# Group 0 of the input projection: the sums of Q5's weights by accumulating transfers in place of additions on VectorE

## The chip, the cores and the metric

The kernel runs on one core of a Trainium2 chip. The metric is the device time of one execution in microseconds. Before the change the median of three runs is 1290.94 us (1290.84 to 1290.96).

The engines are named as the profile names them: PE is TensorE's matmul and PEld its weight load, DVE is VectorE, ACT is ScalarE, POOL is GpSimd, SP is SyncE. POOL and SP, and sometimes ACT, also issue DMA transfers. Each engine works through its own queue in order: an instruction that waits holds up all that stand behind it.

## The reference

The block is one layer of a diffusion transformer over 512 latent tokens of width 2048 and 256 context tokens. One input projection feeds two token mixers, attention and a 2-D Fourier mixing; their gated results are projected, merged with sigmoid gates, projected once more and added to the input. Cut to what matters:

```python
h = _modulate(_rmsnorm(xs, norm_g[l]), shift[:, None], scale[:, None])
p = h @ w_l                                   # (512 x 2048) @ (2048 x 9216)
q = _rope(_rmsnorm(_heads(p, OFF_Q, N_Q_HEADS), q_norm_g[l]), cos, sin) * q_scale
...
attn = _attention(q, jnp.concatenate([k, kc], axis=1), jnp.concatenate([v, vc], axis=1))
y = _merge(p[..., OFF_ZA:], attn, w_proj_a[l], w_proj_b[l], w_out[l])
new_xs = xs + gate[:, None] * y
...
return _rmsnorm(xs, final_g)
```

The change concerns the product h @ w_l, and of its 9216 columns the first 1024 that the kernel's groups work on (512 of the queries, 512 of the gate z_a).

## The kernel before, in words

All inputs are float32. A factor is split into two parts, hi and lo, that TensorE multiplies quickly: ACT copies the source into hi (L180), DVE subtracts hi from the source and gives lo (L181). One product is then three matmuls, hi by hi, lo by hi, hi by lo, on L338, L339 and L340. So the weights of every piece pass through ACT and DVE before TensorE can use them: hi is needed at the first of the three matmuls, lo at the second.

**Stages.** Up to about 144 us the start: adaLN's vectors, the normalized rows h, and the columns of the Fourier branch. To 156 us the Fourier transform along the tokens (tiles ah, al, fch, pd). Then eight groups of the input projection of 76 us and more each, g = 0 to 7, attention from about 810 us, the branch projections, and the output projection.

**A group** is a block product of 1024 columns by seven products instead of eight (a Strassen-Winograd form). h and the weights are cut into 2 x 2 blocks; each product multiplies a form of h (A11, Z5, A12, ...) by a form of the weights. The products run in the order P1, Q5, P2, Q6, P7, Q3, Q4. Each has four pieces of 1024 columns; one piece is 12 matmuls of 128x512. P1, Q5, Q6 and Q4 use running sums of the weight blocks: P1 the first block, Q5 the sum of two, Q6 of three, Q4 of four. P2 and Q3 use one block as it is. P7 uses the sum of three less a block that is loaded for it.

**The chain.** The running sums live in four buffers, R0 to R3, one for each piece (`chain` in the code, R_1339 to R_1342 in the rows below). L219 on SP loads the first block. To add the next block there are two ways:

- L291, a POOL transfer with `accum_op=add`, issued as soon as the piece's split has read R (`e.nxt` in `split_piece`), or
- an addition on DVE, L268, of a raw block that SP has loaded into a buffer wr (L216).

`stream_product` chooses: a step whose number stands in `by_dve` is done on DVE and takes a raw buffer, any other by L291. For the groups `BY_DVE_GATES` is (1,): step 1, from P1's sum to Q5's, is on DVE; the steps to Q6's and, behind P7, to Q4's are on POOL. P7's subtraction is L276: it reads R, which then holds three blocks, and writes the result into the raw buffer.

**Buffers.** There are six raw buffers, four in the pool wp and two in rp, which are handed out again as they come free; three pairs of hi and lo, and from Q5 of group 0 on two more pairs in tiles that h no longer needs (the s tiles 128x2x256 of the rows: s_286/s_287 and s_433/s_434 make up one pair, s_571/s_572 and s_734/s_735 the other).

**Order.** TensorE's order is written out. On DVE, ACT, POOL and SP most of the order of the groups comes from the tile framework's scheduler, which places each instruction by its own estimate of when its inputs are ready. So a change of one step moves others.

**Other work of the stretch.** L966 stores the gates of the Fourier branch (tile part) to memory (b_d) from POOL's queue; L1394 then loads a table into qr, whose memory overlaps that of part, and so waits for both stores. L944 scales the Fourier results into part, L950 and L659 belong to the same stage. L993 and L994 make the forms S2 and S4 of h on DVE. L1106 combines results of the products. L1210 to L1216 rotate the queries.

Of the kernel before, what the change touches and what calls it, by code (L numbers as in the profile page):

```python
# [60 lines left out]
BY_DVE_GATES, BY_DVE_OUT = (1,), ()  # L61
# [11 lines left out]
def context_piece(g, name, pc):  # L73

    n = 28 * (g - NQZ) + 4 * ONE_GROUP.index(name) + pc
    if n % 2 == 0 and 0 <= n < 8:
        return "cn", n // 2
    if n % 7 == 4 and 18 <= n < 46:
        return "cr", n // 7 - 2
# [43 lines left out]
def block_kernel(ctx, tc, xT, ctx_rows, ctx_toks, x, c_row, w_ss, w_gate, vecs, qkg, rope, dft_c, dft_s,  # L123
# [74 lines left out]
    def stream(key, src, *a, **k):  # L198
        todo.append(Piece(key, src if isinstance(src, list) else [src], *a, **k))
# [191 lines left out]
    def stream_product(name, g, w, by_dve, pieces=4):  # L391

        what = next(p[2] for p in PRODUCTS if p[0] == name)
        for pc in range(pieces):
            key = (name, g, pc)
            part = lambda i: w[CHAIN[i][0], CHAIN[i][1], pc]
            r = (pc + CHAIN_FROM.get(g, 0)) % 4
            if isinstance(what, tuple) and name == "P7" and g >= BRANCH_A:
                stream(key, [p7_d[g - BRANCH_A, pc]], 1024, 2, pc=r)
            elif isinstance(what, tuple):  # L400
                off = name == "P7"
                stream(key, [w[a, b, pc] for a, b in what], 1024, 2, pc=r, nxt=part(3) if off else None, off=off)
            else:
                stream(key, [part(what)] if what in by_dve else [], 1024, 2, stage=what, pc=r,
                       nxt=part(what + 1) if what < (3 if g >= BRANCH_A else 2) and what + 1 not in by_dve else None)
                todo[-1].first = part(0)
# [3 lines left out]
    def stream_keys(g):  # L410
        stream(("K", g), flat(k_d[g]), NKEY, KT, "raw")
        stream(("V", g), flat(v_d[g]), NKEY, KT, dst=lambda: tiles(g))
# [8 lines left out]
    for g in range(LAST + 1):  # L421
        for name in ONE_GROUP:
            if (g, name) == (LAST, "Q4"):
                stream_keys(0)
            if g == KV:
                f = CTX_FORMS.index(next(f for n, f, _, _ in PRODUCTS if n == name))
                stream(("cf", name), cf_d[:, :, f].rearrange("i p j c -> p i j c"), 1024, 8, dst=ctx_tiles)
            stream_product(name, g, w_g[g], BY_DVE_GATES)
            for pc in range(4):
                p = context_piece(g, name, pc)  # L430
                if p:
                    src, cols = (ctx_toks[p[1]], 1024) if p[0] == "cn" else (ctx_rows[p[1]], 4 * C)
                    stream(p, src, cols, 1, "raw")
                    todo.insert(len(todo) - 4 + pc, todo.pop())
            for pc in range(4):
                if (g, name, pc) in GATE_AT:
                    q = GATE_AT[g, name, pc]
                    stream(("gate", q), w_gate[q], 1024, 1, "raw")
                    e = todo.pop()
                    at = next(i for i, x in enumerate(todo) if x.key == (name, g, pc))  # L440
                    todo.insert(at + 1, e)
# [1627 lines left out]
```

## Time and profile before

| | us |
|---|---|
| median of 3 runs | 1290.94 |
| the profiled execution | 1290.61 |
| its span | 1288.80 |
| DVE busy | 994.7 (77% of the span) |
| ACT busy | 682.2 (53%) |
| POOL busy | 170.8 (13%) |
| first matmul of group 0 (x, L338) | at 156.13 |
| L268 on DVE, all 32 | 1.22 each |

Times in the rows count from the start of the span. A row of the timeline has the start, the duration, the engine with the line and the operation, out<-in without buffer numbers, the shape, and in brackets the idle time of the engine before it with what ended it. "wr<-in_w_g POOLq ... 512.0 KB, 7.3" in a list of transfers means: so many KB each, and the median time from issue to landing. A waits view says who waited for whom. Matmuls of 128x512 follow each other 0.227 us apart when nothing holds them; a row's own 0.39 us is its passage through the array.

### The profile page before, as it was taken

The page shows a single profiled execution, that of the slowest core. Times are in us where ns is not written, and L with a number is a line of the kernel's source. Part 1 is how long each engine was busy: PE and PEld are TensorE (multiplying, and loading weights), DVE is VectorE, ACT ScalarE, POOL GpSimd, SP SyncE. Part 2 cuts the span into 40 slices and gives each one's busy share as a digit, 9 for nine tenths or more (in the row PEclk, how much of TensorE's full clock was granted, in tenths as well). Part 3 has the DMA queues.
Part 4 walks back from the last instruction along what each step waited for, and adds up shares of the span by engine and source line. Part 5 has one row for each costly group of instructions (what it writes and reads, how often), then busy time and mean ns, then how long its engine had stood idle before and what let it go on. Part 6 is the DMA issues. An engine that isn't in the chain of part 4 may idle for free.

```text
span 1288.8 us, 17680 instructions
## 1 busy us (share of the span) xinstructions
PE 1272.9 (99%) x6586; PEld 1047.9 (81%) x6586; DVE 994.7 (77%) x1305; ACT 682.2 (53%) x1073; POOL 170.8 (13%) x222
## 2 busy tenths in 40 slices
PE   8999999999999999999999999999999999999997
PEld 5677887888888888888888888888888888888886
DVE  5767899889779787658587666788898777887677
ACT  5322654645556555444355544666667646464544
POOL 0000011111102011012031010012100211211210
PEclk9999999999999999999999999999999999999999
DMA  9998588888988988977879897578852989998986
GB/s 378 408 369 344 208 216 248 237 218 261 227 302 236 301 269 260 291 197 184 278 207 259 286 249 237 182 245 241 270 178 75 249 244 258 244 211 229 225 200 179
DMA packets 104486, 319.14 MB, mean 248 GB/s; under 512 B 9904, under 2 KB 33072, under 8 KB 100432
## 3 DMA queue, kind: packets, MB, share of 16 engines
q1 hardware_dynamic: 55056, 197.40, 42.3%
q0 software_dynamic: 27024, 98.19, 35.6%
q10 hardware_dynamic: 22320, 22.42, 5.1%
q8 instruction: 51, 0.84, 0.3%
q14 instruction: 35, 0.29, 0.1%
HBM read 283.36 MB, written 34.61 MB: 247 GB/s over the span
## 4 chain that ended last, share of the span: by engine, by line
PE 91%; DVE 3%; DMA 2%; ACT 2%; issue 1%; SPq 0%; ACTq 0%; DVEq 0%
PE banks L338 10%; PE banks L339 10%; PE banks L340 10%; PE x L340 9%; PE x L338 9%; PE x L339 9%; PE y L340 7%; PE y L339 7%; PE y L338 7%; PE banks L1543 2%; PE pd L566 2%; PE pb L338 1%; PE pb L339 1%; PE pb L340 1%; PE pc L338 1%; DMA wa<-in_w_ss 1%
## 5 line engine op out<-in xcount | busy, mean ns | idle before, releaser
L180 ACT ACTIVATE whi<-R 128x1024 fp32r<-128x1024 f32 x138 | 145.6, 1060 | 142.1 <-PE banks L340 55.3
L181 DVE TENSOR_TENSOR wlo<-R,whi 128x1024 fp32r<-128x1024 f32 x138 | 167.9, 1222 | 57.9 <-ACT whi L180 57.6
L181 DVE TENSOR_TENSOR wlo<-wr,whi 128x1024 fp32r<-128x1024 f32 (+1 forms) x122 | 147.2, 1214 | 63.1 <-ACT whi L180 63.1
L180 ACT ACTIVATE whi<-wr 128x1024 fp32r<-128x1024 f32 (+1 forms) x122 | 127.4, 1052 | 127.3 <-PE y L340 44.3
L338 PE MATMUL banks<-whi,s 128*128 128x512 f32 (+1 forms) x400 | 157.8, 394 | 0.9 <-DVE ev L1106 0.9
L339 PE MATMUL banks<-wlo,s 128*128 128x512 f32 (+1 forms) x400 | 155.8, 389 | 0.0
L340 PE MATMUL banks<-whi,s 128*128 128x512 f32 (+1 forms) x400 | 155.8, 389 | 0.0
L338 PE MATMUL x<-whi,s 128*128 128x512 f32 x352 | 137.1, 390 | 0.0
L340 PE MATMUL x<-whi,s 128*128 128x512 f32 x352 | 137.0, 389 | 0.0
L339 PE MATMUL x<-wlo,s 128*128 128x512 f32 x352 | 136.9, 389 | 0.0
L338 PE MATMUL y<-whi,s 128*128 128x512 f32 x316 | 123.1, 389 | 0.2 <-DVE cxe L1266 0.2
L339 PE MATMUL y<-wlo,s 128*128 128x512 f32 x316 | 123.1, 390 | 0.0
L340 PE MATMUL y<-whi,s 128*128 128x512 f32 x316 | 122.8, 389 | 0.0
L291 POOL DMA_DIRECT2D R<-in_w_g x64 | 56.0, 875 | 415.2 <-DVE wlo L181 212.6
L180 ACT ACTIVATE s<-wr 128x512 fp32r<-128x512 f32 (+2 forms) x93 | 60.9, 678 | 68.1 <-DMA wr<-cf_d 24.9
L338 PEld LDWEIGHTS banks<-whi,s 128*128 128x128 f32 x400 | 75.2, 188 | 16.6 <-DVE ev L1106 1.3
L181 DVE TENSOR_TENSOR s<-wr,s 128x512 fp32r<-128x512 f32 (+2 forms) x93 | 66.7, 750 | 28.3 <-ACT s L180 27.5
L340 PEld LDWEIGHTS banks<-whi,s 128*128 128x128 f32 x400 | 75.1, 188 | 15.3
L339 PEld LDWEIGHTS banks<-wlo,s 128*128 128x128 f32 x400 | 75.2, 188 | 13.6 <-DVE wlo L181 0.2
L340 PEld LDWEIGHTS x<-whi,s 128*128 128x128 f32 x352 | 66.1, 188 | 13.8
L339 PEld LDWEIGHTS x<-wlo,s 128*128 128x128 f32 x352 | 66.1, 188 | 13.7
L338 PEld LDWEIGHTS x<-whi,s 128*128 128x128 f32 x352 | 66.1, 188 | 13.6
(322 smaller groups left out, 2803.2 us busy)
## 6 DMA issues: line engine op xcount, KB each, us to landing
wr<-in_w_g SPq DMA_DIRECT2D x128, 512.0 KB, 5.8
R<-in_w_g POOLq DMA_DIRECT2D x64, 512.0 KB, 7.3
wa<-in_w_ss SPq DMA_DIRECT2D x31, 1024.0 KB, 9.7
R<-in_w_g SPq DMA_DIRECT2D x32, 512.0 KB, 6.0
wr<-in_w_gate SPq DMA_DIRECT2D x32, 512.0 KB, 5.1
wr<-in_w_o SPq DMA_DIRECT2D x24, 512.0 KB, 7.5
R<-in_w_o POOLq DMA_DIRECT2D x24, 512.0 KB, 9.2
wr<-in_w_pab SPq DMA_DIRECT2D x20, 512.0 KB, 6.0
```

Of the source, the lines that this page charges most:

```text
L180: first = nc.scalar.activation(hi, src, ACT.Copy)
L181: return first, nc.vector.tensor_tensor(lo, src, hi.bitcast(F32), op=ALU.subtract)
L291: nc.gpsimd.dma_start(chain[e.pc], e.nxt, accum_op=ALU.add)
L338: nc.tensor.matmul(o, ah, bh, start=start, stop=False, skip_group_check=cont)
L339: nc.tensor.matmul(o, ah, bl, start=False, stop=False, skip_group_check=cont)
L340: nc.tensor.matmul(o, al, bh, start=False, stop=stop, skip_group_check=cont)
L566: nc.tensor.matmul(acc[32 * j : 32 * j + 32], c2[:, n, :], w[:, k, :], start=n < 4, stop=n >= KK - 4)
L1543: nc.tensor.transpose(tp[:, k * P : (k + 1) * P], p[:, k * P : (k + 1) * P], ident)
```

## The change

For group 0 alone, step 1 is no longer given to DVE:

```diff
@@ -425,7 +425,7 @@
             if g == KV:
                 f = CTX_FORMS.index(next(f for n, f, _, _ in PRODUCTS if n == name))
                 stream(("cf", name), cf_d[:, :, f].rearrange("i p j c -> p i j c"), 1024, 8, dst=ctx_tiles)
-            stream_product(name, g, w_g[g], BY_DVE_GATES)
+            stream_product(name, g, w_g[g], BY_DVE_GATES if g else ())
             for pc in range(4):
                 p = context_piece(g, name, pc)
                 if p:
```

In `stream_product` this gives the pieces of P1 of group 0 a `nxt`, an L291 on POOL behind each split, and leaves the pieces of Q5 without a raw block: four loads on SP (L216) and four additions on DVE (L268) go. The raw buffers that Q5 had go to later pieces. TensorE's order is the same, row by row. SP's differs by the four loads. On DVE, ACT and POOL rows move in the stretch from the Fourier stage to the end of group 0; from group 1 on the orders are the same.

The first place is DVE's queue where Q5 is prepared. The names: wlo<-R,whi is the low part of a piece of P1 or Q5, wr_1719 the raw block of P2's third piece, S_67 and S_68 forms of h. Before, from the low part of Q5's second piece on:

```order
L181 TENSOR_TENSOR wlo_1697<-R_1340,whi_1696 128x1024
L181 TENSOR_TENSOR s_572<-wr_1719,s_571 128x2x256
L181 TENSOR_TENSOR s_735<-wr_1719,s_734 128x2x256
L181 TENSOR_TENSOR s_1782<-S_68,s_1781 128x1024
L181 TENSOR_TENSOR wlo_1703<-R_1341,whi_1702 128x1024
L181 TENSOR_TENSOR wlo_1723<-R_1342,whi_1722 128x1024
L993 TENSOR_TENSOR S_67<-s_871,S_67 128x512
```

The same place on DVE with the change, from a split of S_68 through the low part of Q5's first piece (wlo_1669) to that of its third (wlo_1700); wr_1799 is the raw block of P7's first piece:

```order
L181 TENSOR_TENSOR s_1774<-S_68,s_1773 128x1024
L993 TENSOR_TENSOR S_67<-s_871,S_67 128x512
L181 TENSOR_TENSOR wlo_1669<-R_1339,whi_1668 128x1024
L994 TENSOR_TENSOR S_67<-S_67,s_872 128x512
L993 TENSOR_TENSOR S_67<-s_1015,S_67 128x512
L993 TENSOR_TENSOR S_68<-s_1157,S_68 128x512
L181 TENSOR_TENSOR wlo_1695<-R_1340,whi_1694 128x1024
L994 TENSOR_TENSOR S_67<-S_67,s_1016 128x512
L994 TENSOR_TENSOR S_68<-S_68,s_1158 128x512
L993 TENSOR_TENSOR S_68<-s_1241,S_68 128x512
L276 TENSOR_TENSOR wr_1799<-R_1339,wr_1799 128x1024
L181 TENSOR_TENSOR wlo_1700<-R_1341,whi_1699 128x1024
```

The L276 of P7's first piece has moved ahead of the low parts of Q5's third and fourth piece, and so have most of the L993 and L994; P2's splits have moved out, to earlier places.

The second place is POOL's queue behind the Fourier stage. Before:

```order
L766 DMA rot_d<-S_67 128x1024
L966 DMA b_d<-part 128x1024 x2
L1394 DMA qr<-rot_d 128x1024
L291 DMA R_1339<-in_w_g 128x1024
L291 DMA R_1340<-in_w_g 128x1024
```

The same place on POOL with the change; the first L291 of each R is the added one, the second R_1339 is the step to Q6's sum:

```order
L291 DMA R_1339<-in_w_g 128x1024
L291 DMA R_1340<-in_w_g 128x1024
L966 DMA b_d<-part 128x1024
L291 DMA R_1341<-in_w_g 128x1024
L966 DMA b_d<-part 128x1024
L1394 DMA qr<-rot_d 128x1024
L291 DMA R_1342<-in_w_g 128x1024
L291 DMA R_1339<-in_w_g 128x1024
```

Three of the added transfers stand around the two stores, the fourth behind the load of qr, and R_1339's next step behind that.

The third place is DVE's queue at the end of the start, ahead of the Fourier stage. Before:

```order
L181 TENSOR_TENSOR fsq_1348<-wr_1139,fsq_1348 128x512
L659 TENSOR_TENSOR part<-pc_1361,part 128x512
L903 TENSOR_TENSOR u_1375<-pb_296,part 128x512
L903 TENSOR_TENSOR u_1379<-pb_296,part 128x512
L659 TENSOR_TENSOR part<-pc_1383,part 128x512
L950 TENSOR_TENSOR part<-part,e_1479 128x512
```

The same place on DVE with the change; wr_1643 is the raw block of P2's second piece:

```order
L181 TENSOR_TENSOR fsq_1348<-wr_1139,fsq_1348 128x512
L181 TENSOR_TENSOR s_287<-wr_1643,s_286 128x2x256
L181 TENSOR_TENSOR s_434<-wr_1643,s_433 128x2x256
L659 TENSOR_TENSOR part<-pc_1357,part 128x512
L903 TENSOR_TENSOR u_1371<-pb_296,part 128x512
L903 TENSOR_TENSOR u_1375<-pb_296,part 128x512
```

Two splits of P2's second piece have come in ahead of L659; before, they stood in group 0.

## The prediction

> **What bounds the kernel now.** I read the busy shares first, then the waits of TensorE, then the stretch of group 0 by window, then single rows. The page's first and fourth parts:
>
> ```profile
> PE 1272.9 (99%) x6586; PEld 1047.9 (81%) x6586; DVE 994.7 (77%) x1305; ACT 682.2 (53%) x1073; POOL 170.8 (13%) x222
> PE 91%; DVE 3%; DMA 2%; ACT 2%; issue 1%; SPq 0%; ACTq 0%; DVEq 0%
> ```
>
> TensorE (PE) is busy for 99% of the span and is 91% of the chain that ended last. No matmul is added or removed, so time can change only where TensorE waits, and the change touches group 0 alone. Busy time by window (PE, PEld, DVE, ACT, POOL; in brackets the instructions), for group 0 (156 to 232 us) and the group behind it:
>
> ```profile
> 156.00:232.00 76.00, 75.05 (x330) 61.28 (x329) 73.57 (x87) 41.64 (x63) 10.51 (x13) 1.00 0.80 228
> 232.00:308.00 76.00, 76.00 (x337) 62.90 (x337) 66.75 (x79) 40.62 (x77) 11.33 (x12) 1.00 0.89 250
> ```
>
> In 76 us the later group has 337 matmuls, group 0 has 330: about seven matmul slots of 0.227 us, 1.6 us, are missing. VectorE (DVE) is busy for 73.57 of 76 us there, against 66.75 later. So group 0 is where VectorE limits TensorE, by very little. The places are seen in TensorE's timeline, as starts that lie further than 0.227 us apart:
>
> ```profile
> 172.46 0.39 PE L338 MATMUL y<-whi,s 128*128 128x512 f32 x1
> 172.80 0.50 PE L339 MATMUL y<-wlo,s 128*128 128x512 f32 x1
> 173.14 0.40 PE L340 MATMUL y<-whi,s 128*128 128x512 f32 x1
> ...
> 208.06 0.39 PE L338 MATMUL x<-s,s 128*128 128x512 f32 x1
> 209.16 0.50 PE L339 MATMUL x<-s,s 128*128 128x512 f32 x1 [0.71 <-DVE s L181]
> 209.50 0.40 PE L340 MATMUL x<-s,s 128*128 128x512 f32 x1
> ...
> 212.01 0.39 PE L339 MATMUL y<-s,s 128*128 128x512 f32 x1
> 212.64 0.50 PE L340 MATMUL y<-s,s 128*128 128x512 f32 x1 [0.24 <-DVE s L181]
> 212.97 0.39 PE L338 MATMUL y<-s,s 128*128 128x512 f32 x1
> ```
>
> Start to start, less 0.227 each: 172.46 to 173.14 loses 0.22 us (third piece of Q5, waiting for wlo), 208.06 to 209.50 loses 0.98 (last piece of P7), 212.01 to 212.97 loses 0.50 (Q3). Together **1.70 us**, which is all that group 0 can give back; 1.48 of it lies in the two later places.
>
> **What is removed.** Four additions on VectorE and the four SP loads that fed them:
>
> ```profile
> L268 DVE TENSOR_TENSOR R<-R,wr x4: 1218/1221/1221, 156.0 to 164.0; 128x1024 f32<-128x1024 f32 x4
> 157.69 2.35 DVE L181 TENSOR_TENSOR s<-Z,s 128x1024 fp32r<-128x1024 f32 x2
> 173.79 1.29 DVE L993 TENSOR_TENSOR S<-s,S 128x512 f32<-128x512 f32 x2
> ```
>
> Two instructions of 1024 columns take 2.35 us with one tail of 1.22, so in a full queue one costs 1.13 us; of 512 columns 0.60. VectorE is given 4 x 1.13 = 4.5 us. That is more than the 1.70 us that TensorE waits, so by itself it would clear all three places. The late subtraction behind the second place is seen here, between work that is less urgent:
>
> ```profile
> 205.55 1.22 DVE L276 TENSOR_TENSOR wr<-R,wr 128x1024 f32<-128x1024 f32 x1
> 206.68 1.22 DVE L1106 TENSOR_TENSOR ev<-ev,ev 128x1024 f32<-128x1024 f32 x1
> 207.81 2.50 DVE L181 TENSOR_TENSOR s<-wr,s 128x512 fp32r<-128x512 f32 x4
> ```
>
> In the changed order this fourth L276 stands ahead of the rotation (L1210 to L1216) and not behind it, so I take both later waits as gone: minus 1.48 us. If they stayed, 1.48 us would come back.
>
> **What is moved early.** The freed buffers take P2's second piece at once, and its two splits of 512 columns now stand ahead of the last sum of the start (L659). The load in that place of SP's queue starts at 132.44 and takes 3.6 us; VectorE and ScalarE sat idle there anyway:
>
> ```profile
> wr<-in_w_g SPq DMA_DIRECT2D x1, 512.0 KB, 3.6
> 136.64 0.69 DVE L659 TENSOR_TENSOR part<-pc,part 128x512 f32<-128x512 f32 x1 [1.69 <-PE pc L340]
> 139.36 0.69 DVE L659 TENSOR_TENSOR part<-pc,part 128x512 f32<-128x512 f32 x1 [0.83 <-PE pc L340]
> 140.39 0.69 DVE L950 TENSOR_TENSOR part<-part,e 128x512 f32<-128x512 f32 x1 [0.34 <-ACT e L949]
> 137.35 1.06 ACT L180 ACTIVATE whi<-R 128x1024 fp32r<-128x1024 f32 x1 [2.46 <-DMA R<-in_w_g]
> ```
>
> The piece is there at 136.04, ScalarE is done with both halves at about 137.3, just as R0 comes in, and VectorE at 138.0. L659 starts 1.3 us later than now, and the idle 0.83 and 0.34 behind it absorb that until 140.4. I cost this at nothing. The cover is those 1.17 us of idle time; if the load were a microsecond later, the Fourier stage would start late by as much.
>
> **What is added: a wait in VectorE's queue.** This is the term that decides. In the changed order the first L276 (P7's first piece, wr_1799 from R0) stands directly ahead of the low splits of Q5's third and fourth piece (wlo_1700, wlo_1717); now it stands 18 rows behind the first of them. It reads R0 after three sums, so it needs R0's *second* accumulating transfer, which can only start when Q5's first piece has been split, and VectorE works in order. When does VectorE get there?
>
> ```profile
> 157.09 0.69 DVE L944 SCALAR_TENSOR_TENSOR part<-pd,part 128x512 f32<-128x512 f32 x1
> 165.18 1.22 DVE L181 TENSOR_TENSOR wlo<-R,whi 128x1024 fp32r<-128x1024 f32 x1
> ```
>
> The last L944 starts at 157.09 now, behind an L268; I put it at 156.6. From there the changed rows are: L944 and one P2 split (2 x 0.60), the two Z splits, one S split, the low part of P1's fourth piece and the other S split (5 x 1.13), one L993 (0.60). That is 156.6 + 1.2 + 5.65 + 0.6 = 164.05 for the low part of Q5's first piece (now 165.18), done at 165.3. From there that one itself (1.13), three of 512 (1.8), the low part of Q5's second piece (1.13) and three of 512 (1.8): VectorE stands at L276 at about **170.0**, with nothing else it may do.
>
> When does R0 land? POOL's queue now and the time from issue to landing, first of the two b_d stores, then of the first L291, then of the two at 188 and 190:
>
> ```profile
> 153.66 0.53 POOL L966 DMA_DIRECT2D b_d<-part  x1 [74.20 <-DVE part L944]
> 158.07 0.53 POOL L966 DMA_DIRECT2D b_d<-part  x1 [3.88 <-DVE part L944]
> 162.48 0.55 POOL L1394 DMA_DIRECT2D qr<-rot_d  x1 [3.87 <-ACT whi L180]
> 166.70 0.90 POOL L291 DMA_DIRECT2D R<-in_w_g  x1 [3.68 <-DVE wlo L181]
> ...
> 188.38 0.86 POOL L291 DMA_DIRECT2D R<-in_w_g  x1 [13.35 <-DVE wr L276]
> 190.12 0.86 POOL L291 DMA_DIRECT2D R<-in_w_g  x1 [0.88 <-DVE wr L276]
> ```
>
> ```profile
> b_d<-part POOLq DMA_DIRECT2D x1, 512.0 KB, 2.9
> b_d<-part POOLq DMA_DIRECT2D x1, 512.0 KB, 3.8
> R<-in_w_g POOLq DMA_DIRECT2D x1, 512.0 KB, 8.6
> R<-in_w_g POOLq DMA_DIRECT2D x1, 512.0 KB, 5.5
> R<-in_w_g POOLq DMA_DIRECT2D x1, 512.0 KB, 6.8
> R<-in_w_g POOLq DMA_DIRECT2D x1, 512.0 KB, 11.5
> ```
>
> The qr load starts at 162.48, 0.6 us after the second b_d store has landed (158.07 + 3.8 = 161.9). It keeps waiting for that store, and R3's first accumulation is queued behind it. The store itself now comes behind R2's accumulation (issued at about 156.3, landing 5.5 later at 161.8), so I let it land at 163.5, qr start at 164.1, R3 at 164.8 and R0's second at **165.7** (Q5's first split at 165.3 allows it, with 0.3 of release as now from 166.40 to 166.70). Alone such a transfer takes 5.5 us, so R3 lands at 170.3; the pair at 188.38 and 190.12 landed at 193.9 and 196.9, 3.0 apart, so R0 lands at 173.3, say **173.4**. The first row of 8.6 us shared the engines with SP's loads; 11.5 is the last of four in a row. In the changed order SP has few loads here: six raw pieces fetch early, one (wr_1821) at about 158, the next only when P2's first piece has been split, which is behind L276. So I stay near the 5.5 and 3.0 rows and keep 8.6 and 11.5 for the upper end.
>
> Then L276 takes 1.13, wlo_1700 1.22, with 0.1 of release: the low half is there at 175.85, where the L339 at 172.80 could start. TensorE stands until then: **plus 3.05 us**. Behind it, wlo_1717 is done 1.13 later, before TensorE's next piece (12 x 0.227 = 2.7 us later). P7's other subtractions wait for R1 to R3, which land at 176 to 185, before they are needed in front of 200. Sum: 3.05 - 1.48 = **+1.6 us** (the 0.22 at 172.8 is paid either way). In one formula: the change is R0's landing minus 171.8.
>
> One page of the Trainium skill speaks about the term of 5.5 us: "DMA: Bandwidth & Descriptors", section "Anatomy of one DMA — SWDGE (gpsimd) path", fits a transfer as 2.0 us plus bytes over 436 GB/s, 3.2 us for 512 KB. By that figure R0 would land near 169.3 and the wait would not exist. The plain b_d store agrees with it (2.9); the accumulating L291 does not (5.5 at its quietest here), and I go by the L291 row.
>
> **The rivals.** *Slower by more than 0.2%:* the same wait at L276, but R0 lands late because the accumulations crowd each other and wr_1821, as they do now at 166.70 (8.6 us). From 165.7 that is 174.3, a change of +2.5 us; with 9.5 us it is +3.4, with 11.5 it is 177.2 and +5.4. It decides from a landing at 174.4 on. For it speaks that four POOL transfers stand in one queue; against it the missing SP loads. *No wait at all:* the accumulations are as quick as a plain transfer of the same queue (2.9 us), R0 lands before 170.3, when L276 and wlo_1700 would still be in time for 172.7, and all 1.70 us are won: 1290.94 - 1.7 = 1289.2 us. Against it speak all L291 rows. *The later waits stay:* VectorE saves 4.5 us but stands idle 3.4 at L276, so it is only 1.1 us ahead; if that is not enough at 208, 1.48 comes on top, 1294.0 us. *The change does not do what it says* I exclude: in the order four L268 are gone and four L291 added.
>
> **How the numbers follow.** The profiled execution took 1290.61 us, a span of 1288.80 and 1.81 around it; plus 1.6 gives 1292.2. The median of three is 0.33 higher, so I predict **1292.5 us**. About 0.2% (2.6 us) is what a measurement of this kernel can tell from no change. Chances: forecast (+0.2 to +2.6) 0.58; slower rival with late landing 0.22; later waits stay 0.07, most of it beyond 2.6; the wait small or absent (below +0.2) 0.13, of which hardly any gets below -2.6, since only 1.70 can be won. So faster 0.02, within 0.2% 0.70, slower 0.28. The range runs from a landing at 171.5 (-0.3) to one at 176.2 (+4.4): 1290.6 to 1295.3.
>
> **What would show it.** In the changed profile: VectorE idle before an L276 near 170 to 173, released by a DMA into R; TensorE idle for some 3 us at an L339 of tile y near 173 to 176, by a wlo split; no waits near 209 and 213; POOL's R3 accumulation directly behind qr; the last fch matmul still near 156. I am wrong if R0's second accumulation lands before 170 or after 175, if L659 or L950 start later than now, or if TensorE waits at a place in another group.

## The result, and the profile after

The changed kernel takes **1300.08 us** (median of 6 runs, 1298.54 to 1302.45) against 1290.95 for the kernel before (6 runs, 1290.84 to 1292.13): a ratio of 1.007, 95% interval 1.006 to 1.0079. It is 9.1 us slower; the forecast was 1292.5 us, 1.6 us slower, with a range up to 1295.3. The profiled execution took 1298.9 us, a span of 1297.1, which is 8.3 more than the profiled execution before.

First the same window view as in the prediction: group 0 and the group behind it, then the ten microseconds in the middle of group 0 and the four behind those (length, PE, PEld, DVE, ACT, POOL busy with their instructions, granted clock, DMA share, GB/s):

```profile
156.00:232.00 76.00, 67.45 (x291) 55.37 (x290) 61.58 (x72) 35.91 (x54) 12.38 (x15) 0.93 0.81 204
232.00:308.00 76.00, 76.00 (x337) 62.94 (x336) 65.44 (x78) 41.37 (x77) 11.33 (x12) 1.00 0.85 239
172.00:182.00 10.00, 1.45 (x6) 0.89 (x5) 3.18 (x3) 2.00 (x2) 0.52 (x1) 0.64 0.79 151
182.00:184.00 2.00, 2.00 (x7) 1.52 (x6) 2.00 (x4) 1.04 (x1) 1.19 (x2) 0.50 0.53 66
184.00:186.00 2.00, 2.00 (x8) 1.63 (x7) 2.00 (x3) 0.12 (x2) 0.00 (x0) 0.73 1.06 195
```

Group 0 has 291 matmuls where it had 330; the next group has 337 as before. Most of the loss is in one place: between 172 and 182 us TensorE works for 1.45 of 10 us. And behind that gap there is a second loss which the busy time hides: from 182 to 184 PE is busy for all of 2.00 us, but only five matmuls start in it where nine fit at 0.227 (the 7 of the row are those that reach into the window), at a granted clock of 0.50. TensorE's timeline shows both (start, duration):

```profile
172.30 0.39 PE L338 MATMUL y<-whi,s 128*128 128x512 f32 x1
181.24 0.80 PE L339 MATMUL y<-wlo,s 128*128 128x512 f32 x1 [8.55 <-DVE wlo L181]
181.83 0.63 PE L340 MATMUL y<-whi,s 128*128 128x512 f32 x1
182.26 0.63 PE L338 MATMUL y<-whi,s 128*128 128x512 f32 x1
...
184.82 0.51 PE L338 MATMUL y<-whi,s 128*128 128x512 f32 x1
185.17 0.40 PE L339 MATMUL y<-wlo,s 128*128 128x512 f32 x1
```

Start to start less 0.227, as in the prediction: 172.30 to 181.24 loses 8.71 us, at the first L339 of Q5's third piece, the place that the forecast named. From 181.24 to 185.17 stand nine steps of 0.35 to 0.59, seven of them 0.43, which lose another 1.90. Together 10.61 us against the 1.70 of before. The waits at 209 and 212.6 are gone, as forecast: no start from 207 to 214 is further than 0.23 from the one ahead.

What TensorE waited for is seen on VectorE:

```profile
167.95 1.29 DVE L994 TENSOR_TENSOR S<-S,s 128x512 f32<-128x512 f32 x2
169.15 0.70 DVE L993 TENSOR_TENSOR S<-s,S 128x512 f32<-128x512 f32 x1
178.82 1.23 DVE L276 TENSOR_TENSOR wr<-R,wr 128x1024 f32<-128x1024 f32 x1 [8.97 <-DMA R<-in_w_g]
179.97 2.35 DVE L181 TENSOR_TENSOR wlo<-R,whi 128x1024 fp32r<-128x1024 f32 x2
```

VectorE is done with everything ahead of L276 at 169.85 and stands there until R0's second accumulating transfer lands at 178.8. The low split behind L276, which reads a buffer that has long been ready, starts at 179.97. POOL's queue shows why R0 was late (the instruction's start, what it waited for), and the rows below it the time from issue to landing:

```profile
156.42 0.85 POOL L291 DMA_DIRECT2D R<-in_w_g  x1 [2.05 <-ACT s L180]
157.38 0.56 POOL L966 DMA_DIRECT2D b_d<-part  x1
167.77 0.55 POOL L1394 DMA_DIRECT2D qr<-rot_d  x1 [9.82 <-DMA b_d<-part]
168.31 2.72 POOL L291 DMA_DIRECT2D R<-in_w_g  x3
```

```profile
R<-in_w_g POOLq DMA_DIRECT2D x1, 512.0 KB, 9.5
b_d<-part POOLq DMA_DIRECT2D x1, 512.0 KB, 9.8
qr<-rot_d POOLq DMA_DIRECT2D x1, 512.0 KB, 3.7
R<-in_w_g POOLq DMA_DIRECT2D x1, 512.0 KB, 8.0
```

The first two of the lower rows belong to R2's accumulation at 156.42 and the second b_d store at 157.38, the last to R3's accumulation at 168.31. R2's accumulation took 9.5 us, not 5.5; the store behind it 9.8, so it landed at 167.2, not 163.5. The load of qr waits for that store, and three accumulations (R3, R0, R1) wait behind qr and are then issued at once; R3 lands at 176.3 and R0, 2.5 us behind, at 178.8.

### The profile page after: what moved, and what is told of

Read it like the earlier page. It is cut to its first block, busy times and chain, and to the rows that moved or that the text cites. A ratio compares the mean times of both kernels' runs of the same rounds, so it can differ in the third digit from the quotient of the medians.

```text
span 1297.1 us, 17685 instructions
## 1 busy us (share of the span) xinstructions
PE 1272.8 (98%) x6586; PEld 1048.6 (81%) x6586; DVE 991.4 (76%) x1301; ACT 682.0 (53%) x1073; POOL 172.9 (13%) x226
## 4 chain that ended last, share of the span: by engine, by line
PE 91%; DMA 3%; ACT 2%; DVE 2%; issue 1%; POOL 0%; SPq 0%; POOLq 0%; DVEq 0%; ACTq 0%
PE banks L338 10%; PE banks L339 10%; PE banks L340 10%; PE x L339 8%; PE x L340 8%; PE x L338 8%; PE y L339 8%; PE y L340 8%; PE y L338 8%; PE banks L1543 2%; PE pd L566 2%; PE pb L338 1%; PE pb L339 1%; PE pb L340 1%; PE pc L338 1%; PE pc L340 1%
## 5 line engine op out<-in xcount | busy, mean ns | idle before, releaser
L339 PE MATMUL banks<-wlo,s 128*128 128x512 f32 (+1 forms) x400 | 155.8, 389 | 0.0
L339 PE MATMUL x<-wlo,s 128*128 128x512 f32 x352 | 137.1, 389 | 0.2 <-DVE wlo L181 0.2
L339 PE MATMUL y<-wlo,s 128*128 128x512 f32 x316 | 123.8, 392 | 8.6 <-DVE wlo L181 8.6
L291 POOL DMA_DIRECT2D R<-in_w_g x68 | 59.2, 887 | 487.1 <-DVE wlo L181 226.7
L339 PEld LDWEIGHTS banks<-wlo,s 128*128 128x128 f32 x400 | 75.3, 188 | 13.8 <-DVE wlo L181 0.2
L339 PEld LDWEIGHTS x<-wlo,s 128*128 128x128 f32 x352 | 66.1, 188 | 14.3 <-DVE wlo L181 0.6
L339 PEld LDWEIGHTS y<-wlo,s 128*128 128x128 f32 x316 | 59.8, 189 | 21.4 <-DVE wlo L181 9.0
L338 PEld LDWEIGHTS x<-whi,s 128*128 128x128 f32 x352 | 66.1, 188 | 13.6
```

The costliest lines, as they stand in the source:

```text
L291: nc.gpsimd.dma_start(chain[e.pc], e.nxt, accum_op=ALU.add)
L338: nc.tensor.matmul(o, ah, bh, start=start, stop=False, skip_group_check=cont)
L339: nc.tensor.matmul(o, ah, bl, start=False, stop=False, skip_group_check=cont)
```

## Experiments

All times below are medians, compared with runs of the kernel before on the same chip in the same session (medians 1290.78 to 1290.83; three sessions, each on another chip). "Lost" is read from TensorE's starts in group 0 of the profiled execution, start to start less 0.227, summed over all steps that lose more than 0.06.

**Four kernels that take the cause apart.** The first moves one row of VectorE:

```diff
...
-                if e.key[1] in DIFF_IN_LINE:
+                if e.key == ("P7", 0, 0) or e.key[1] in DIFF_IN_LINE:
+                    behind = split_of[-2] if e.key[1] in DIFF_IN_LINE else lows[("Q5", 0, 3)]
-                    line.enter_context(tc.issue_after(split_of[-2][1].ins))
+                    line.enter_context(tc.issue_after(behind[1].ins))
...
-        split_of.append(last_split[-1])
+        split_of.append(last_split[-1]); lows[e.key] = last_split[-1]
```

> The changed kernel with one row moved: the first L276 (P7's first piece, wr_1799 from R0) stands behind the low split of Q5's fourth piece on VectorE; POOL's and SP's queues are as in the changed kernel. Theory A (the place of L276 in VectorE's queue turns R0's late landing into TensorE's wait): R0's landing at about 178.8 no longer matters to Q5's third piece. What is left is R3's first accumulation, landing at about 176.3 as in the changed kernel: ScalarE's high half 1.06 later, the low half 1.22 behind that, against a need at 175.0, so TensorE stands some 3.5 us at Q5's fourth piece. 3.5 - 1.7 = +1.8, so 1292.7 us, and up to 2 us more if the matmuls behind the wait run at the lower clock again. Theory B (the accumulations are too slow for this place wherever L276 stands; the wait only moves on to the next piece and keeps its size): 1298 to 1300 us.

Measured: 1294.37 us (10 runs), ratio 1.0025 (1.0016 to 1.0035). The profile has the wait where theory A put it, now at Q5's fourth piece and for R3:

```profile
174.99 0.39 PE L340 MATMUL y<-whi,s 128*128 128x512 f32 x1
177.69 0.50 PE L338 MATMUL y<-whi,s 128*128 128x512 f32 x1 [2.31 <-ACT whi L180]
178.95 0.50 PE L339 MATMUL y<-wlo,s 128*128 128x512 f32 x1 [0.76 <-DVE wlo L181]
```

The two steps lose 2.48 and 1.03, 3.51 us where 3.5 was expected; the matmuls behind run at 0.43 us again and lose 1.7. So R0's late landing costs what it did because the L276 that reads it stands ahead of the split that TensorE needs. With the row moved, the fourth accumulation itself is still too late for its piece: order is the larger part of the loss (5.6 of the 9.1 us), not all of it.

The second leaves the order and moves the three other POOL transfers to SP's queue:

```diff
-        nc.gpsimd.dma_start(b_d[i], part[:, 4 + 2 * i : 6 + 2 * i, :])
+        nc.sync.dma_start(b_d[i], part[:, 4 + 2 * i : 6 + 2 * i, :])
...
-    nc.gpsimd.dma_start(turning, rot_d)
+    nc.sync.dma_start(turning, rot_d)
```

> The changed kernel with the two b_d stores (L966) and the load of qr (L1394) issued by SP in place of POOL; VectorE's order, with L276 ahead of Q5's low splits, is as in the changed kernel. Theory Q (R3's first and R0's second accumulation were late because they stood in POOL's queue behind qr, which waits for the second b_d store): R3 is issued at about 162.5 and R0 at 165.3 in place of 168.3 and 168.9; each takes the 5.5 us of a quiet one, R0 lands near 171 to 172, and by the formula 'landing minus 171.8' the time is 1290 to 1291.5 us. Theory C (the accumulations crowd one another and the other transfers in the DMA engines, whatever queue they stand in): R0 still takes 9.9 us from 165.3, lands at 175.2, +3.4 plus the slower matmuls behind the wait, 1294 to 1297 us. If neither counts, 1300 us as the changed kernel.

Measured: 1293.72 us (10 runs, 1291.3 to 1296.96), ratio 1.0022 (1.0013 to 1.0031). On VectorE:

```profile
169.64 0.68 DVE L993 TENSOR_TENSOR S<-s,S 128x512 f32<-128x512 f32 x1
173.78 1.22 DVE L276 TENSOR_TENSOR wr<-R,wr 128x1024 f32<-128x1024 f32 x1 [3.46 <-DMA R<-in_w_g]
```

R0's second accumulation is issued at 165.9 and lands at 173.8, between the two theories: 7.9 us on the way. Of the 5.0 us that it lands earlier, 3.0 are the earlier issue (168.9 to 165.9) and 2.0 the shorter way (9.9 to 7.9; it no longer starts together with two others). TensorE loses 3.20 us in the wait, and 2.91 in 14 slow steps behind it.

The third has both edits.

> The changed kernel with both edits: L276 behind the low split of Q5's fourth piece, and the b_d stores and the load of qr on SP. Theory A with Q: R3's first accumulation is issued near 162.5 and lands by 170 to 172.5, before Q5's fourth piece needs it (173.9 for no wait), nothing stands ahead of Q5's low splits, and the 1.70 us that TensorE loses in group 0 before the change are gone: 1289.2 us. Theory A with C: R3 lands at 172.5 to 174, a wait of 0 to 0.5 us, 1289 to 1290 us. Theory B: above 1293 us.

Measured: **1288.3 us** (11 runs), ratio 0.9979 (0.9970 to 0.9988). The window view of group 0:

```profile
156.00:232.00 76.00, 76.00 (x338) 63.02 (x337) 71.86 (x84) 41.32 (x61) 11.08 (x13) 1.00 0.89 230
```

TensorE is busy for all of the 76 us, with 338 matmuls. Theory B falls here: accumulating transfers for all four pieces are quick enough if nothing stands in front of them and nothing urgent behind them.

The fourth undoes half of the change: accumulating transfers for Q5's first two pieces, additions for the others.

```diff
-    def stream_product(name, g, w, by_dve, pieces=4):
+    def stream_product(name, g, w, all_dve, pieces=4, adds=range(4)):
...
-            key = (name, g, pc)
+            key, by_dve = (name, g, pc), all_dve if pc in adds else ()
...
-            stream_product(name, g, w_g[g], BY_DVE_GATES if g else ())
+            stream_product(name, g, w_g[g], BY_DVE_GATES, adds=range(4) if g else (2, 3))
```

> Accumulating transfers for Q5's first two pieces alone; the third and fourth keep their additions on VectorE (two L268, two SP loads). In this order L276 of P7's first piece stands behind all of Q5's low splits, and POOL's queue holds two accumulations ahead of the b_d stores and none between them and qr. Theory A/Q: no wait at Q5; VectorE saves 2 x 1.13 = 2.3 us, which is more than the 1.70 us that TensorE loses before the change, but the two later places need the order behind P7 to be better as well: 1289.2 to 1290.9 us. Theory B or C: the two accumulations delay the stores and qr, R0's next step lands late, 1292 us and more.

Measured: 1288.29 us (11 runs), ratio 0.9979 (0.9970 to 0.9988), a little under what was expected, and nothing lost in group 0. The second b_d store, without R2's accumulation ahead of it, takes 6.4 us in place of 9.8 and lands at 163.6:

```profile
b_d<-part POOLq DMA_DIRECT2D x1, 512.0 KB, 6.4
```

**Which part of POOL's queue.** Only the load of qr goes to SP (the second of the two lines above):

> The changed kernel with the load of qr (L1394) alone on SP; the b_d stores stay on POOL, VectorE's order stays as changed. Theory Q (qr, waiting for the second b_d store, holds up R3's and R0's accumulations behind it in POOL's queue): R3 issued near 162.8 and R0 near 165.9 in place of 168.3 and 168.9, R0 lands near 174 as with all three moved, TensorE stands some 3.2 us and runs 2 to 3 us behind at the lower clock: 1293 to 1295 us. Rival (the stores in POOL's queue are as much to blame): R0 issued at 168 or lands at 177 and later, 1297 us and more.

Measured: 1295.13 us (9 runs, 1291.32 to 1296.48), ratio 1.003 (1.002 to 1.0039). POOL's rows:

```profile
162.55 0.86 POOL L291 DMA_DIRECT2D R<-in_w_g  x1 [4.57 <-DVE wlo L181]
165.42 0.86 POOL L291 DMA_DIRECT2D R<-in_w_g  x1 [2.01 <-DVE wlo L181]
```

R3 and R0 are issued as soon as VectorE has split the piece ahead, and R0 lands at 172.8. TensorE loses 2.68 in the wait and 1.7 behind it. So it was qr alone, waiting for the second store, that held the accumulations up. (The median is a little over theory Q's range. What group 0 loses in the profiled execution, on top of the 1288.4 of a kernel that loses nothing there, explains 1292.8; the runs of this kernel lie 5 us apart.)

Then three accumulations, with the addition kept for Q5's third piece, so that R2's accumulation is the one that goes (`adds=range(4) if g else (2,)`):

> Accumulating transfers for Q5's pieces 1, 2 and 4; the third piece alone keeps its addition on VectorE (one L268, one SP load). In this order L276 of P7's first piece stands behind Q5's low splits, and R2's accumulation no longer stands between the two b_d stores. Theory C (R2's accumulation, crowding the second b_d store, made that land at 167.2, not 163.5): the store lands at 163.6 as it did with two accumulations, qr at 164.2, R3 at 164.8, landing 8.3 us later at 173.1, just before 173.9: no wait or a few tenths, 1288.3 to 1289 us. Rival (the store is slow because of R0's and R1's accumulations): the store lands at 167, R3 at 176.4, TensorE stands 3.5 us and runs 1.7 us behind, 1293.5 us.

Measured: 1290.57 us (11 runs), ratio 0.9996 (0.9987 to 1.0005): no difference. The store lands at 163.9, as theory C had it, and qr is issued at 164.45. But R3's accumulation took 9.4 us, and not 8.3:

```profile
164.45 0.55 POOL L1394 DMA_DIRECT2D qr<-rot_d  x1 [6.48 <-PE x L340]
164.98 1.83 POOL L291 DMA_DIRECT2D R<-in_w_g  x2
```

```profile
qr<-rot_d POOLq DMA_DIRECT2D x1, 512.0 KB, 3.8
R<-in_w_g POOLq DMA_DIRECT2D x1, 512.0 KB, 9.4
```

It lands at 174.35, 0.45 behind the 173.9 that would have been in time, and TensorE loses 1.55 us at Q5's fourth piece (0.52 for the high half, 1.03 for the low), as much as it saves elsewhere (1.67 lost in group 0, against 1.70 before). R2's accumulation is shown to be what made the store late; the time of an accumulation behind it was again set too low by me: 8.3 was its time in the kernel with the moved row, where no load of SP ran beside it, and here one was issued at 165.8. That this load is what made it slower was not tested. (The page names PE as what ended qr's wait; the store's landing, 0.56 us earlier, fits the other runs too.)

**The slow matmuls behind the wait.** The changed kernel, with 33 matmuls of zero weights put into the wait; they add zero to the sums:

```diff
-        nc.tensor.matmul(o, ah, bh, start=start, stop=False, skip_group_check=cont)
+        nc.tensor.matmul(o, ah, bh, start=start, stop=False, skip_group_check=cont); [nc.tensor.matmul(o, zero, bh, start=False, stop=False, skip_group_check=cont) for _ in range(spare.pop() if spare else 0)]
...
+                spare.extend([33] if (name, self.g, pc) == ("Q5", 0, 2) else [])
```

> The changed kernel with 33 more matmuls (zero weights, into the same bank, 33 x 0.227 = 7.5 us) between the first L338 and the first L339 of Q5's third piece, that is inside the 8.6 us in which TensorE stood; nothing else in the queues changes up to there. Theory K (the long idle itself made the next eight matmuls run at the 0.43 us pitch and the lower granted clock, a loss of 1.9 us): they now run at 0.227, the clock of the group stays at 1.00, the start of the L339 stays near 181, and the time falls by 1.9 us against the changed kernel, to 1297 to 1298.2 us. Rival (the slow pitch comes from the transfers or the late splits, not from TensorE's idling): pitch 0.43 and 1299 to 1300 us as before. If 33 matmuls were longer than the wait, the time would rise by the rest.

Measured: 1299.43 us (5 runs), ratio 1.0069 (1.0056 to 1.0082). The time hardly falls, but the timeline is clear:

```profile
172.78 7.86 PE L338 MATMUL y<-whi,zero 128*128 128x512 f32 x33
181.85 0.50 PE L339 MATMUL y<-wlo,s 128*128 128x512 f32 x1 [1.21 <-DVE wlo L181]
182.19 0.39 PE L340 MATMUL y<-whi,s 128*128 128x512 f32 x1
182.42 0.40 PE L338 MATMUL y<-whi,s 128*128 128x512 f32 x1
```

```profile
156.00:232.00 76.00, 74.61 (x329) 60.98 (x328) 62.26 (x74) 35.75 (x55) 12.35 (x15) 1.00 0.79 203
```

With the gap filled, the steps behind it are 0.23 us at once, and the clock of the group is 1.00 (0.93 without). Theory K holds for the mechanism. The gain in time is smaller than it said: R0 landed 0.6 us later in this execution (179.4), and a new loss of 0.45 us stands at 198, where VectorE's order had shifted. Filling, waits and all, group 0 loses 9.4 us here, 1.2 less than without the filling; the medians, 0.65 apart, could not have shown it by themselves.

The same with 12 such matmuls in the kernel that has the stores and qr on SP:

> The kernel with all three transfers (b_d stores, qr) on SP and L276 still ahead, with 12 more matmuls of zero weights (2.7 us) inside the wait of 3.0 to 3.2 us at Q5's third piece. Theory K: the 2.9 us that it lost to matmuls at 0.43 us pitch are gone, only the wait is left: 1288.3 (no loss in group 0) + 3.2 = 1291.5 us, which is the size that the forecast gave the wait. Rival: 1293.7 us as without the matmuls.

Measured: 1292.41 us (11 runs), ratio 1.0014 (1.0005 to 1.0023). The slow steps are gone here too: the wait and the filling together lose 4.3 us, against 6.1, although R0 landed at 175.1 in this execution, later than the 173.8 on which I had built. That is what shows theory K a second time. The times alone would not: the median is 1.3 us lower than without the matmuls, but the intervals of the two ratios overlap. It is also 0.9 above what was expected, and that stays open, since the profiled execution was the slowest of the eleven (1294.39 us) and its late landing need not be that of the others.

**Two kernels forecast from the theory that was left.** First the moved row of VectorE together with qr alone on SP:

> The changed kernel with L276 behind the low split of Q5's fourth piece and the load of qr alone on SP; the b_d stores stay on POOL. If the order of VectorE and the place of qr in POOL's queue are the whole cause, R3 is issued near 162.6, lands by 170 to 171, Q5 waits for nothing, no matmul runs at the lower clock, and the time is 1288.3 us, as with the stores moved too. If the stores in POOL's queue still cost something, R3 lands after 173.9 and the time is 1290 us or more.

Measured: 1288.5 us (11 runs), ratio 0.9983 (0.9974 to 0.9992). R3 is issued at 162.8 and lands at 169.8; nothing is lost in group 0. Second, the addition kept for Q5's fourth piece alone (`adds=range(4) if g else (3,)`):

> Accumulating transfers for Q5's first three pieces; the fourth alone keeps its addition on VectorE. In this order L276 of P7's first piece stands behind all of Q5's low splits; R2's accumulation still stands between the two b_d stores, so the second store lands at 167 and qr and R0's next step are as late as in the changed kernel (R0 landing 177 to 179). If a late landing costs only where something urgent stands behind it on VectorE or waits for R3, TensorE waits for nothing here: 1288.3 to 1289 us. Rival (the late R0 costs by itself, in Q6 or P7): 1290.5 us and more.

Measured: 1288.23 us (11 runs), ratio 0.9981 (0.9972 to 0.9990). R0 lands at 178.7, as late as in the changed kernel, and it costs nothing, since L276 stands behind Q5's splits and VectorE comes to it only at 179.65:

```profile
172.77 1.22 DVE L181 TENSOR_TENSOR wlo<-R,whi 128x1024 fp32r<-128x1024 f32 x1
173.91 1.28 DVE L994 TENSOR_TENSOR S<-S,s 128x512 f32<-128x512 f32 x2
175.11 1.21 DVE L181 TENSOR_TENSOR wlo<-wr,whi 128x1024 fp32r<-128x1024 f32 x1
176.25 2.35 DVE L181 TENSOR_TENSOR s<-S,s 128x1024 fp32r<-128x1024 f32 x2
178.51 1.22 DVE L181 TENSOR_TENSOR wlo<-wr,whi 128x1024 fp32r<-128x1024 f32 x1
179.65 2.35 DVE L276 TENSOR_TENSOR wr<-R,wr 128x1024 f32<-128x1024 f32 x2
```

All but the two kernels with filled waits in one table (waits and slow steps of the profiled executions, in us; "late" is the landing that TensorE had to wait for):

| kernel | late | lost in waits | lost in slow steps | median |
|---|---|---|---|---|
| before | none at Q5 | 1.70 | 0 | 1290.8 to 1290.95 |
| changed | R0, 178.8 | 8.71 | 1.90 | 1300.08 |
| L276 behind the splits | R3, 176.5 | 3.51 | 1.72 | 1294.37 |
| stores and qr on SP | R0, 173.8 | 3.20 | 2.91 | 1293.72 |
| qr on SP | R0, 172.8 | 2.68 | 1.71 | 1295.13 |
| piece 3 by addition | R3, 174.35 | 1.55 | 0.11 | 1290.57 |
| L276 moved, stores and qr on SP | none | 0 | 0 | 1288.30 |
| L276 moved, qr on SP | none | 0 | 0 | 1288.50 |
| pieces 3 and 4 by addition | none | 0 | 0 | 1288.29 |
| piece 4 by addition | none | 0 | 0 | 1288.23 |

The last four are faster than both kernels, by 2.3 to 2.5 us against before. No run took the order alone, an early L276 in the kernel that still has its four additions, so what the order would cost without the added transfers stays open.

## Why the prediction was wrong, step by step

- *What bounds the kernel, and what can be won (1.70 us)*: right. Four kernels without a wait in group 0 end 2.3 to 2.5 us below the kernel before. 1.70 of that is group 0's loss; between 235 and 700 us the kernel before also loses 0.69 against 0.09 in three of the four. The few tenths left are not traced.
- *The additions removed, the later waits gone (minus 1.48)*: right, no wait is left at 209 and 212.6. The rival that these would stay is out.
- *P2's second piece moved early, at no cost*: right. L659 starts at 137.71 (136.64 before), L950 at 140.15 (140.39), and TensorE is busy for all of 144 to 156 in both. (The prediction names a later L659 among the signs of being wrong, though it had itself put L659 1.3 us later; it came 1.07 later, at no cost, so that sign says nothing.)
- *VectorE stands at L276 from 170.0 on*: right, 169.85. The place, the releaser and the kind of wait were right too: "the same wait", TensorE at an L339 of y, waiting for a low split that stands behind L276. With the landing put in, the formula holds: 178.8 + 1.13 + 1.22 + 0.1 gives 181.25, and the L339 started at 181.24.
- *"R0 lands at 173.3, say 173.4"*: **this is the term that failed**; it measured 178.8, beyond the 175 that the prediction had named as the sign of being wrong. It failed in two links of the same chain. I let R2's accumulation land 5.5 us after its issue, at 161.8, and with it the second b_d store at 163.5; they measured 165.9 and 167.2, so qr, R3 and R0 were issued 3.2 to 3.7 us late. Without R2's accumulation the store does land at 163.6 and 163.9: the step from store to qr to R3 was sound, the 5.5 in front of it was not. And I gave R3 5.5 us on the way, with R0 3.0 behind it; R3 took 8.0 and R0 landed 2.5 behind it, because by the time that qr was out three accumulations were ready and started together, right behind qr's own load. (In the five kernels with qr on SP, where R3 is issued 2.9 us ahead of R0, it took 6.4 to 7.5.) 3.5 of later issue, 2.5 on R3's way, less 0.5 between R3 and R0: 5.5, against the 5.4 that R0 was late. The 5.5 was the row of a lone transfer. The rows of 8.6 and 11.5, which I kept for the upper end, were the ones of transfers in company, and company was what the change brought.
- *The rival "R0 lands late, they crowd each other"* was the right mechanism with too short a reach: it let the crowding begin at R0, from 165.7, and not at R2, issued nine microseconds earlier. Its worst case was 177.2.
- *A cost that the prediction did not have*: the matmuls behind the wait ran at half clock, 1.90 us. Its first step, that "time can change only where TensorE waits", left this out: these matmuls lose time while TensorE is busy. All the waits of group 0 before the change are under 1 us and show nothing of it.

In sum, against the profiled execution before: 8.71 + 1.90 lost, 1.70 no longer lost, plus 8.9 in group 0 for 8.3 in the span; the medians lie 9.1 apart. The forecast had 3.27 (3.05 and the 0.22 that is paid either way) in place of the 8.71, and nothing in place of the 1.90. The kernel with the stores and qr on SP comes near the forecast's own case, by another queue: R0 lands at 173.8, TensorE loses 3.20 in the wait, close to the 3.27 worked out, and the term that was missing is seen by itself: 2.91 us at half clock in the profiled execution. In the median that kernel is slower by 2.9 us, and not by 1.6.

The Trainium skill, "DMA: Bandwidth & Descriptors", section "Anatomy of one DMA — SWDGE (gpsimd) path", fits a transfer of POOL's path as 2.0 us plus bytes over 436 GB/s, which makes an estimate of 3.2 us for 512 KB. No run here shows an accumulating transfer as quick: the quickest L291 in the whole trace of the changed kernel took 5.2, and the rows decide. (With 3.2, R0 would land at 165.7 + 3.2 = 168.9 and not at the 169.3 of the prediction; both lie before 170.3, so nothing hangs on it.)

## What to carry to other kernels

Work taken off an engine and given to a queue of transfers is priced by what that queue and the DMA engines hold at that moment, not by the row of a transfer that ran alone; follow the queue from the first added transfer on, since each link passes its delay to the next. Where freed buffers let a scheduler fetch later work early, look for what that work puts at the head of an in-order engine: here one subtraction, wanted more than 20 us later, stood in front of a split wanted at once, and one forced order took 5.6 of the 9.1 us back. If a wait of several microseconds can't be excluded on TensorE, add the slow matmuls behind it to its price.

## What the runs showed of the hardware

**An accumulating transfer occupies the DMA engines twice as long as a plain one of the same queue and size.** Rows of POOL's queue (packets, MB, share of the 16 engines' time): the changed kernel from 172 to 178 us, where only accumulations run, and the kernel before from 154.5 to 156.3, where the first b_d store is alone:

```profile
q0 software_dynamic: 301, 1.13, 99.3%
```

```profile
q0 software_dynamic: 144, 0.52, 72.9%
```

99.3% of 6 us for 1.13 MB is 5.3 us of all sixteen engines per MB; 72.9% of 1.8 us for 0.52 MB is 2.5. That store writes to memory, while an accumulation loads from it, so the direction could be the reason as well. Plain loads settle this: in the kernel before, from 20 to 60 us, SP's loads fill the engines,

```profile
q1 hardware_dynamic: 2671, 16.35, 100.0%
```

which is 40 us for 16.35 MB, 2.4 us per MB (though by SP's queue). A piece of 512 KB (0.52 MB) thus takes 2.8 us of all the engines when it accumulates, which is about the 2.5 to 3.0 us by which neighbours in a row landed apart. So a further accumulation adds its full time once the engines are full: three issued 0.57 us apart land 2.5 us apart, 8.0, 9.9 and 11.8 us after their issue.

**Half clock after a gap.** Steps of 0.43 us in place of 0.227 followed gaps on TensorE in group 0 of 8.55, 3.04, 2.52 and 2.31 us (the last with one of 0.76 behind it), for 3.3 to 6.1 us of time; gaps of 1.21 us and less (two kernels with filled waits, the one with piece 3 by addition, and the kernel before) had none. The loss did not grow with the gap: 2.91 us behind the gap of 3.04, 1.90 behind that of 8.55. The granted clock (third figure from the end of a row) says why. First two windows of the changed kernel, then two of the kernel with the stores and qr on SP:

```profile
174.00:175.00 1.00, 0.00 (x0) 0.00 (x0) 0.00 (x0) 0.00 (x0) 0.00 (x0) 0.91 0.98 184
185.00:186.00 1.00, 1.00 (x6) 0.82 (x5) 1.00 (x2) 0.11 (x1) 0.00 (x0) 0.97 1.10 225
```

```profile
175.00:176.00 1.00, 0.00 (x0) 0.00 (x0) 1.00 (x2) 0.00 (x0) 0.00 (x0) 0.70 0.27 49
182.00:183.00 1.00, 1.00 (x6) 0.82 (x5) 0.98 (x2) 0.41 (x1) 0.00 (x0) 0.89 1.12 221
```

A mean of 0.91 over 1 us is 0.18 us at 0.50, so the clock of the changed kernel fell at 174.8, inside the gap, and was back at 185.1; in the other it was 0.50 from 175.4 to 182.2. Read in the same way, it was 0.50 from 175.7 to 179.1 with qr alone on SP, and from 179.4 to 182.8 with L276 moved. The four lengths, 10.2, 6.8, 3.4 and 3.4 us, are three, two, one and one times 3.4, and the loss is about half of what lies behind the gap: 3.8 of the 10.2 us in the changed kernel (the rest passed while TensorE stood), 6.0 of the 6.8 in the other.

In the kernel with qr on SP the first two matmuls behind the gap were still quick and the slow ones followed:

```profile
175.23 0.50 PE L339 MATMUL y<-wlo,s 128*128 128x512 f32 x1 [2.52 <-DVE wlo L181]
175.57 0.52 PE L340 MATMUL y<-whi,s 128*128 128x512 f32 x1
175.88 0.63 PE L338 MATMUL y<-whi,s 128*128 128x512 f32 x1
176.31 0.63 PE L339 MATMUL y<-wlo,s 128*128 128x512 f32 x1
```

The Trainium skill, "TensorE: Matmul & The Clock Gate", section "What's actually happening", has the clock halved after an idle window of about 3.4 us and given back after as long a busy one, in windows that run on by themselves. The half clock, its lengths in steps of 3.4 us and the start of the slow steps some way behind the gap agree with that; the length of the idle time does not, since gaps of 2.3 and 2.5 us were enough here.
